# Order of the three partial products in a block product, of low parts and joins on VectorE, and the place of the sinks' load in a hybrid attention and recurrence block

## The chip, the cores and the metric

The kernel runs on one core of one Trainium2 chip. The metric is the device time of one execution in microseconds (us); a lower time is better. Five engines work side by side and meet through semaphores: TensorE (PE, its weight loads PEld), VectorE (DVE), ScalarE (ACT), GpSimd (POOL) and SyncE (SP), which issues most DMAs. Each works through its own queue in order.

## The reference

One residual block of a decoder, 1024 tokens by 1024 channels, in float32. The part that takes most of the time is one input projection onto 6656 columns; its output is cut into attention (q, k, v), a recurrence (xr), two SiLU gates and two merge gates.

```python
h = rmsnorm(x, norm_g[l]) * (1.0 + scale[:, None, :]) + shift[:, None, :]
proj = h @ w_in[l]
q, k, v, g_attn, xr, g_rnn, m_attn, m_rnn = jnp.split(proj, SPLIT_POINTS, axis=-1)
...
y_attn = sliding_window_attention_with_sinks(q, k, v, attn_sinks[l]) * jax.nn.silu(g_attn)
xr = causal_depthwise_conv(xr, conv_w[l], conv_b[l])
y_rnn = rg_lru(xr, positions, rg_wa[l], rg_ba[l], rg_wx[l], rg_bx[l], rg_lambda[l]) * jax.nn.silu(g_rnn)
merged = (jax.nn.sigmoid(m_attn) * (y_attn @ w_attn_proj[l])
          + jax.nn.sigmoid(m_rnn) * (y_rnn @ w_rnn_proj[l]))
x = x + gate[:, None, :] * (merged @ w_out[l])
return rmsnorm(x, final_g)
```

The attention is over blocks of 128 tokens with 16 heads, a window of 128, and one learned sink for each head: the sink is one more logit in the maximum and in the denominator of the softmax, without a value.

```python
m = jnp.maximum(jnp.max(s, axis=-1, keepdims=True), sink)
p = jnp.exp(s - m)
denom = jnp.sum(p, axis=-1, keepdims=True) + jnp.exp(sink - m)
```

## The kernel before

**Arithmetic.** Every large matrix is split into a high part, a float32 rounded to TensorE's fp32r form, and a low part, the rest. A product is then three matmuls: high by high, low weight by high, high weight by low. For a tile of weights the high part `wh` is a cast on ScalarE (`cast`, L105, L107), the low part `wl` a subtraction on VectorE (`rest`, L111, L113) that reads `wh`. Both come from a ring of five buffers (`slot`).

**Input projection by block products.** Most of the projection is done in 23 pairs of 128-column chunks. A `Pair` is a 2 by 2 block product in seven multiplications instead of eight (Strassen's scheme in Winograd's form): sums S1 to S4 of the four weight blocks A11, A12, A21, A22 (`tsum`, L732, VectorE), and prepared sums of the activations. Each of the seven is one call of `product` (L703 to L712): four slices of 128 along the contraction, three matmuls each, twelve matmuls of 128x512 into one PSUM bank, all with their own weight load. The loop is over slices on the outside, and inside it takes high weights by high activations, low weights by high activations, high weights by low activations. The first matmul of a product needs `wh`, the second `wl`.

**Slots.** `run` (L843) walks a table of slots; a slot is one product on TensorE. After the product of slot t has been issued, the steps that were put down for t are issued in the order in which they were put there: weight loads, casts, sums, low parts, copies out of the banks, joins, sinks. A step is a tuple of its engine, its times for ScalarE and VectorE, and a function; the letter is not used for anything else. Behind them `background` issues steps of the recurrence, the rope tables and w_out as far as its estimate of each engine's load allows. The order in each engine's queue is the order of these calls (`manual_schedule`); only the output stage at the end is ordered by the scheduler, after its own model of the time.

**Joins.** The seven products of a pair accumulate in four banks bk0 to bk3. C11 is read as it stands (`b1`), with a bank copy on ScalarE (L762); C12 and C22 are differences of a bank and a block kept in SBUF (`join`, L770, VectorE). A join waits for TensorE's product, and what stands behind it in VectorE's queue waits with it. The join of C12 reads the bank of product S4 (sixth of a pair), which the next pair's S1 (its second) overwrites; the join of C22 reads the bank of S3 (seventh), into which A22 adds in the next pair's third slot. What a pair's output is for decides the steps after a join ("sinks" of a pair, not to be confused with attention's): rope for q, tanh and a product (L830) for gates, convolution for xr.

**Attention.** After the last pair but one, `open_attn` opens new pools in memory that the recurrence has left, loads keys, queries, the sinks (16 numbers to all partitions, issued by GpSimd) and values, and 32 units follow, one for each key-value group and block of 128 tokens, interleaved with the last pair's seven products and then with the recurrence's projection. For a unit u: GpSimd copies four sinks into the last column of the tile `p` (`sink`, L1315); TensorE makes the scores (L1327); ScalarE copies them beside the sinks (L1336); VectorE merges the window (L1342), or for the first block of a group GpSimd masks it (L1345, select); VectorE takes the negative maximum (L1347); ScalarE the exponentials (L1352); then the division, transposes, splits and values.

**Constants.** `pk_t` (128 x 96) holds small columns for every channel, loaded at the start. Its columns 8 to 15 (`PK_BSH`) and 16 to 23 (`PK_BSC`) are the biases of shift and scale; they are read in the start stage alone, by `scales_of` and by one sum into `bng`.

The tile names of the profile: `bk` a bank, `wh`, `wl` the parts of weights, `r` a raw weight tile, `ws` a sum of blocks, `hh`, `hl`, `nh`, `nl` the parts of activations, `c` an output block, `u`, `p` kept blocks (`p` is attention's tile too), `s_ps` scores.

Of the kernel before, what the change touches and what calls it, by code (L numbers as in the profile page):

```python
# [12 lines left out]
F32 = mybir.dt.float32  # L13
# [9 lines left out]
P = 128  # L23
S = 1024
D = 1024
KC = 8
HALF = 512
NH = 16
# [26 lines left out]
def tile_hybrid_block(ctx, tc, x, pk, rows, posr, posi, c_row, w_ss, w_gate, w_main, w_v,  # L55
# [53 lines left out]
    def rest(dst, src, scale=1.0):  # L109
        if scale == 1.0:  # L110
            V.tensor_tensor(out=dst[1][:], in0=src, in1=f32(dst[0][:]), op=ALU.subtract)  # L111
        else:
            V.scalar_tensor_tensor(out=dst[1][:], in0=src, scalar=scale, in1=f32(dst[0][:]),  # L113
                                   op0=ALU.mult, op1=ALU.subtract)
# [463 lines left out]
    W = {}  # L578
# [78 lines left out]
    fixed = {}  # L657
# [46 lines left out]

    def product(ps, w, b, first=True):
        h, l = w
        for kc in range(4):
            c = slice(kc * P, (kc + 1) * P)
            for i, (ww, xx_) in enumerate(((h, 0), (l, 0), (h, 1))):
                W["pe"] = T.matmul(ps, ww[:, c], b[kc][xx_],  # L710
                                   start=(first and kc == 0 and i == 0),
                                   stop=(kc == 3 and i == 2), skip_group_check=not first)  # L712

    class Pair:
        def __init__(self, c, sinks, scale=1.0):
# [2 lines left out]
        def place(self, s, par, last):  # L718

            b1, b2, b3 = bk[0], bk[1 + par], bk[3]  # L720
            R, O, sc = {}, {}, self.scale
            self.ops, self.banks = O, (b1, b2, b3, bk[2 - par])

            def load(n):
                i, j = int(n[1]) - 1, int(n[2]) - 1
                return "S", 0, 0, lambda: R.__setitem__(
                    n, load_half(w_main[self.c + i][:, SL[j]]))

            def tsum(dst, a, b, op):
                def f():  # L730
                    R[dst] = wp.tile([P, HALF], F32, tag="ws", name="ws", bufs=3)[:]
                    V.tensor_tensor(out=R[dst], in0=R[a], in1=R[b], op=op)  # L732
                return "D", 0, 0.69, f

            def hi(n):
                def f1():
                    O[n] = slot()
                    cast(O[n], R[n], sc)
                return "A", 0.62, 0, f1

            def lo(n):
                return "D", 0, 0.69, lambda: rest(O[n], R[n], sc)

            SUB, ADD = ALU.subtract, ALU.add
            at_slot(s - 6, [load("A11"), load("A21")], load("A22"), load("A12"))
            at_slot(s - 2, [hi("A11"), tsum("S1", "A21", "A22", ADD)],
                    [hi("S1"), lo("A11"), tsum("S2", "S1", "A11", SUB)],
                    [lo("S1"), tsum("S3", "A21", "A11", SUB)],
                    hi("S2"),
                    [hi("A12"), lo("S2"), tsum("S4", "S2", "A12", SUB)],  # L750
                    [hi("S4"), lo("A12")], [hi("S3"), lo("S4")], lo("S3"))
            at_slot(s + (5 if last else 7), hi("A22"), lo("A22"))

            T_ = {}

            def keep(n, src):
                def f():
                    T_[n] = stp.tile([P, HALF], F32, tag=n, name=n)
                    A.copy(T_[n][:], src)
                return "A", 0.58, 0, f  # L760

            at_slot(s + 1, ("A", 0.58, 0, lambda: A.copy(b1, b2)))  # L762
            at_slot(s + 2, keep("p5", b3))
            at_slot(s + 4, keep("u2", b2))
            at_slot(s + 5, *self.sinks["C11"](lambda: b1))

            def join(out_, n, a, b):
                def f():
                    T_[n] = out_()
                    V.tensor_tensor(out=T_[n], in0=a(), in1=b(), op=SUB)  # L770
                return "D", 0, 0.69, f

            d12, k12 = self.sinks["C12"]
            d22, k22 = self.sinks["C22"]
            at_slot(s + 6, join(d12, "C12", lambda: T_["u2"][:], lambda: b3),
                    *k12(lambda: T_["C12"]))
            at_slot(s + 7, join(d22, "C22", lambda: b2, lambda: T_["p5"][:]),
                    *k22(lambda: T_["C22"]))
            if last:
                def add():  # L780
                    V.tensor_tensor(out=T_["u2"][:], in0=T_["u2"][:], in1=self.banks[3], op=ADD)
                at_slot(s + 7, keep("u2", b2), ("D", 0, 0.69, add),
                        *self.sinks["C21"](lambda: T_["u2"][:]))
            else:
                at_slot(s + self.sinks.get("late", 10), *self.sinks["C21"](lambda: b2))
# [61 lines left out]
    def run(pairs, extra):  # L847

        n = len(pairs)
        for t in range(-6, 7 * n + 14):  # L850
            i, k = divmod(t, 7)
            q = {0: (0, "A11", B11, 1, True), 1: (0, "S1", NT1, 2, True),
                 2: (-1, "A22", NT4, 1, False), 3: (0, "S2", T2, 1, False),
                 4: (0, "A12", B21, 0, False), 5: (0, "S4", B22, 2, False),
                 6: (0, "S3", NT3, 1, False)}[k]
            if t == 7 * n:
                q = -1, "A22", NT4, 3, True
            d = 0.0
            if 0 <= i + q[0] < n and t <= 7 * n:
                d = extra()  # L860
                p = pairs[i + q[0]]
                product(p.banks[q[3]], p.ops[q[1]], q[2], q[4])
                d += SLOT
            W["slot"] = t
            for st_ in fixed.pop(t, ()):
                put(st_)
            if d:
                background(d)
                Load.pe += d
            if d or t > 7 * n:  # L870
                yield
# [404 lines left out]
    def open_attn():  # L1276
        nonlocal at, psx
        psm_ctx.close()
        psx = pool(psx_ctx, "psx", space=PSUM)
        W["kq"] = pool(at_ctx, "kq", bufs=2, side="right")  # L1280
        W["yo"] = pool(at_ctx, "yo", side="right")
        W["pp"] = pool(at_ctx, "pp", bufs=3, side="right")
        W["pp"].tile([P, 56], F32, name="pad", bufs=1)
        at = pool(at_ctx, "at", side="right")
        load_kq(0)
        W["sink"] = W["pp"].tile([P, NH], F32, name="sink", bufs=1)
        dma(W["sink"][:], rows[0:1, 2048:2048 + NH].to_broadcast([P, NH]), G)
        load_v(0)
        load_kq(1)

# [21 lines left out]
    def sink(u):  # L1312
        px = U["p", u] = W["pp"].tile([P, 4, P + 1], F32, tag="p", name="p")
        gs = slice(u // 8 * 4, u // 8 * 4 + 4)
        G.tensor_copy(px[:, :, P:P + 1], W["sink"][:, gs].unsqueeze(2))  # L1315

    def scores(u):
        g, n = u // 8, u % 8
# [320 lines left out]
    b12_ctx.close()  # L1639
    Load.act = Load.dve = 0.0  # L1640

    W["vpp"] = pool(rope_ctx, "vp", side="right")
    for g in range(NG):
        v_prep(g)
# [397 lines left out]
```

## Time and profile before

| | |
|---|---|
| three timed runs | 914.56, 915.07, 917.21 us, median 915.07 |
| the profiled execution | 917.52 us, its span 915.8 us |
| granted TensorE clock, mean | 0.997 |
| matmuls, of them in block products | 4259, 1932 |
| TensorE's matmuls busy | 899.3 us, 98% |
| VectorE busy | 717.0 us, 78% |
| ScalarE busy | 566.0 us, 62% |
| GpSimd busy | 130.5 us, 14% |
| DMA, mean over the span | 197 GB/s |

The span goes from the first to the last instruction; the execution's own time has 1.7 us more around it. The stages follow one another: start and norm up to about 60 us, the first projections and v up to 92, the block products of 23 pairs up to about 592 with the recurrence between them, attention from 564 to 740 with the recurrence's projection between its units, the attention projection and the merge up to 832, then the output projection and the last norm. In a row of a timeline the columns are start, duration, engine, line, operation, output and inputs, shapes and count; the bracket at the end is the idle time of that engine ahead of the row and who ended it. In a row of waits they are who waited, for whom, and then the total, the count and the longest.

### The profile page before, as it was taken

What the parts mean: (1) busy time and instruction counts of PE and PEld (TensorE: products, weight loads), DVE (VectorE), ACT (ScalarE), POOL (GpSimd) and SP (SyncE); (2) the same over time, 40 slices, a digit from 0 to 9 for tenths busy, and PEclk for the clock granted to TensorE, in tenths of its full rate; (3) what the DMA queues carried; (4) which work ended last, traced back from release to release, by engine and by line L of the source; (5) the groups of instructions that cost most, each with busy time, mean ns of one, the idle gap of its engine ahead of it and who ended that gap; (6) DMA issues with size and microseconds to landing.
All of it is one profiled execution on the core that took longest, in us unless ns stands there. A gap on an engine that the chain in (4) does not pass through costs nothing.

```text
span 915.8 us, 12572 instructions
## 1 busy us (share of the span) xinstructions
PE 899.3 (98%) x4259; PEld 745.9 (81%) x4259; DVE 717.0 (78%) x1071; ACT 566.0 (62%) x1102; POOL 130.5 (14%) x216
## 2 busy tenths in 40 slices
PE   8999999999999999999999999999999999999996
PEld 6789888788888788878888887888888888888885
DVE  6997687888669865987788596899999946678855
ACT  7965554645566755776495884788888733115435
POOL 6520241200000000000000001253444400000000
PEclk9999999999999999999999999999999999999999
DMA  9828489772435353353546257996665279416504
GB/s 356 330 77 274 171 266 302 242 237 94 149 127 190 129 199 120 127 185 123 173 154 211 104 177 264 309 384 240 196 216 204 93 284 378 142 46 230 207 1 184
DMA packets 87204, 180.72 MB, mean 197 GB/s; under 512 B 8626, under 2 KB 29122, under 8 KB 87140
## 3 DMA queue, kind: packets, MB, share of 16 engines
q1 hardware_dynamic: 83056, 167.07, 51.9%
q0 software_dynamic: 3936, 12.59, 4.4%
q8 instruction: 33, 0.54, 0.2%
q14 instruction: 31, 0.25, 0.1%
q10 hardware_dynamic: 148, 0.27, 0.1%
HBM read 121.34 MB, written 58.95 MB: 197 GB/s over the span
## 4 chain that ended last, share of the span: by engine, by line
issue 44%; PE 41%; DVE 9%; ACT 3%; DMA 2%; POOL 1%; SPq 0%; DVEq 0%; POOLq 0%; ACTq 0%
PE rp L173 13%; PE out L1855 6%; PE pmain L173 5%; PE bk L710 4%; PE s_ps L1327 3%; PE pv L1400 2%; PE pmain L485 2%; PE bk L485 2%; PE pt L1366 1%; DMA wr<-w_gate 1%; PE pmain L1577 1%; PE pmain L1576 1%; PE pmain L1575 1%; DVE wl L113 1%; DVE wl L111 1%
## 5 line engine op out<-in xcount | busy, mean ns | idle before, releaser
L710 PE MATMUL bk<-nh,wl 128*128 128x512 f32 x368 | 144.4, 392 | 2.8 <-DVE wl L111 2.8
L710 PE MATMUL bk<-nh,wh 128*128 128x512 f32 x368 | 144.1, 392 | 0.0
L710 PE MATMUL bk<-nl,wh 128*128 128x512 f32 x368 | 143.9, 391 | 0.0
L111 DVE TENSOR_TENSOR wl<-r,wh 128x512 fp32r<-128x512 f32 x109 | 78.9, 731 | 8.7 <-ACT wh L105 8.7
L710 PEld LDWEIGHTS bk<-nh,wl 128*128 128x128 f32 x368 | 69.5, 189 | 19.0 <-DVE wl L111 4.4
L105 ACT CAST wh<-r 128x512 fp32r<-128x512 f32 x107 | 65.6, 618 | 30.6 <-PE rp L173 10.0
L710 PEld LDWEIGHTS bk<-nh,wh 128*128 128x128 f32 x368 | 69.5, 189 | 14.5 <-ACT bk L762 0.2
L710 PEld LDWEIGHTS bk<-nl,wh 128*128 128x128 f32 x368 | 69.4, 189 | 14.3
L710 PE MATMUL bk<-hh,wl 128*128 128x512 f32 x184 | 72.1, 392 | 0.4 <-DVE wl L111 0.4
L710 PE MATMUL bk<-hl,wh 128*128 128x512 f32 x184 | 71.6, 389 | 0.0
L710 PE MATMUL bk<-hh,wh 128*128 128x512 f32 x184 | 71.6, 389 | 0.0
L111 DVE TENSOR_TENSOR wl<-ws,wh 128x512 fp32r<-128x512 f32 x76 | 51.9, 684 | 4.0 <-ACT wh L105 4.0
L62 POOL DMA_DIRECT2D yh_d<-av x1 | 0.6, 567 | 373.9 <-ACT av L1086 373.9
L1352 ACT ACTIVATE p<-p,small 128x129 f32<-128x129 f32 x128 | 50.1, 401 | 0.3 <-DVE small L1347 0.3
L105 ACT CAST wh<-ws 128x512 fp32r<-128x512 f32 x76 | 46.0, 614 | 3.3 <-PE bk L710 2.1
L710 PEld LDWEIGHTS bk<-hh,wl 128*128 128x128 f32 x184 | 34.5, 188 | 9.0 <-DVE wl L111 1.5
L710 PEld LDWEIGHTS bk<-hh,wh 128*128 128x128 f32 x184 | 34.5, 188 | 7.1
L710 PEld LDWEIGHTS bk<-hl,wh 128*128 128x128 f32 x184 | 34.5, 188 | 7.0
L1327 PE MATMUL s_ps<-ks,qs 128*128 128x256 f32 (+1 forms) x256 | 37.6, 289 | 0.4 <-DMA qs<-q_d 0.2
L710 PE MATMUL bk<-hha,wl 128*128 128x512 f32 x92 | 36.2, 393 | 1.7 <-DVE wl L111 1.0
L823 ACT ACTIVATE c<-bk 128x512 f32<-128x512 f32 x29 | 17.3, 596 | 31.2 <-PE bk L710 31.2
L710 PE MATMUL bk<-hha,wh 128*128 128x512 f32 x92 | 35.9, 390 | 0.0
(375 smaller groups left out, 2321.3 us busy)
## 6 DMA issues: line engine op xcount, KB each, us to landing
r<-w_main SPq DMA_DIRECT2D x100, 256.0 KB, 4.4
wada<-w_ss SPq DMA_DIRECT2D x16, 512.0 KB, 9.0
qs<-q_d SPq DMA_DIRECT2D x16, 512.0 KB, 5.5
wo_d<-wr SPq DMA_DIRECT2D x28, 256.0 KB, 2.8
wo<-wo_d SPq DMA_DIRECT2D x14, 512.0 KB, 5.5
ks<-k_d SPq DMA_DIRECT2D x12, 384.0 KB, 4.3
xt<-x SPq DMA_DIRECT2D x8, 512.0 KB, 7.2
sma_d<-c SPq DMA_DIRECT2D x16, 256.0 KB, 4.7
```

Of the source, the lines that this page charges most:

```text
L105: A.copy(dst[0][:], src)
L111: V.tensor_tensor(out=dst[1][:], in0=src, in1=f32(dst[0][:]), op=ALU.subtract)
L113: V.scalar_tensor_tensor(out=dst[1][:], in0=src, scalar=scale, in1=f32(dst[0][:]), op0=ALU.mult, op1=ALU.subtract)
L173: mm = T.matmul(ps[hf], ww, xx[kc][hf], start=(kc == 0 and ww is w_h and xx is xh), stop=(kc == KC - 1 and xx is xl))
L485: T.matmul(starts[c][hf], ww[:, c0:c0 + P], xh[kc][hf], start=(kc == 0 and t_ == "h"), stop=(kc == KC - 1 and t_ == "l"))
L710: W["pe"] = T.matmul(ps, ww[:, c], b[kc][xx_], start=(first and kc == 0 and i == 0), stop=(kc == 3 and i == 2), skip_group_check=not first)
L823: A.activation(t["t"], s(), AF.Tanh, scale=0.5)
L1327: W["pe"] = T.matmul(o, qs[:, j, qc], ks[:, kb:n % 2 + 2, b, :], start=(b == 0), stop=(b == 1))
L1352: A.activation(px[:, j, :], px[:, j, :], AF.Exp, bias=sm[:, 0, j:j + 1], accum_out=sm[:, 1, j:j + 1])
L1366: W["pe"] = T.transpose(pt[:, j, :], px[:, j, 0:P], ident[:])
L1400: W["pe"] = T.matmul(pv[:], b, m[:].rearrange("p j q -> p (j q)"), start=(i == 0), stop=(i == len(prods) - 1))
L1855: T.matmul(o, a[k][x_][:, p * P:(p + 1) * P], b[k][y_][:, cols], start=(first and k == 0 and i == 0), stop=(k == 3 and i == 2), skip_group ...
```

## The change

Three edits. `product` runs the high weights over all four slices first, each slice with the high and then the low part of the activations, and then the low weights over the four slices: the first eight matmuls need `wh` only, the last four `wl`. `lo`, the step that makes a low part, gets the letter "L" for "D", and `run` sorts the steps of a slot so that those with "L" come first, all others in their old order. The sinks are loaded right after the start stage into columns 8 to 23 of `pk_t`, and attention copies them from there; the tile `sink` is gone, and a pad of 56 columns ahead of attention's tiles grows by its 16 columns to 72, so that the other tiles stay where they were.

```diff
     def product(ps, w, b, first=True):
         h, l = w
-        for kc in range(4):
-            c = slice(kc * P, (kc + 1) * P)
-            for i, (ww, xx_) in enumerate(((h, 0), (l, 0), (h, 1))):
-                W["pe"] = T.matmul(ps, ww[:, c], b[kc][xx_],
-                                   start=(first and kc == 0 and i == 0),
-                                   stop=(kc == 3 and i == 2), skip_group_check=not first)
+        terms = [(h, kc, i) for kc in range(4) for i in range(2)] + [(l, kc, 0) for kc in range(4)]
+        for n, (ww, kc, i) in enumerate(terms):
+            W["pe"] = T.matmul(ps, ww[:, kc * P:(kc + 1) * P], b[kc][i],
+                               start=(first and n == 0), stop=(n == 11),
+                               skip_group_check=not first)
...
             def lo(n):
-                return "D", 0, 0.69, lambda: rest(O[n], R[n], sc)
+                return "L", 0, 0.69, lambda: rest(O[n], R[n], sc)
...
             W["slot"] = t
-            for st_ in fixed.pop(t, ()):
+            for st_ in sorted(fixed.pop(t, ()), key=lambda s_: s_[0] != "L"):
                 put(st_)
...
-        W["pp"].tile([P, 56], F32, name="pad", bufs=1)
+        W["pp"].tile([P, 72], F32, name="pad", bufs=1)
         at = pool(at_ctx, "at", side="right")
         load_kq(0)
-        W["sink"] = W["pp"].tile([P, NH], F32, name="sink", bufs=1)
-        dma(W["sink"][:], rows[0:1, 2048:2048 + NH].to_broadcast([P, NH]), G)
         load_v(0)
...
-        G.tensor_copy(px[:, :, P:P + 1], W["sink"][:, gs].unsqueeze(2))
+        G.tensor_copy(px[:, :, P:P + 1], pk_t[:, PK_BSH:PK_BSH + NH][:, gs].unsqueeze(2))
...
     b12_ctx.close()
     Load.act = Load.dve = 0.0
 
+    dma(pk_t[:, PK_BSH:PK_BSH + NH], rows[0:1, 2048:2048 + NH].to_broadcast([P, NH]), G)
     W["vpp"] = pool(rope_ctx, "vp", side="right")
```

On TensorE, a product of the last pair, between the scores (`s_ps`) of attention's second and third unit; before:

```order
L710 MATMUL bk_69<-nh_751,wh 128x512
L710 MATMUL bk_69<-nh_751,wl 128x512
L710 MATMUL bk_69<-nl,wh 128x512
L710 MATMUL bk_69<-nh_752,wh 128x512
L710 MATMUL bk_69<-nh_752,wl 128x512
L710 MATMUL bk_69<-nl,wh 128x512
L710 MATMUL bk_69<-nh_753,wh 128x512
L710 MATMUL bk_69<-nh_753,wl 128x512
L710 MATMUL bk_69<-nl,wh 128x512
L710 MATMUL bk_69<-nh_754,wh 128x512
L710 MATMUL bk_69<-nh_754,wl 128x512
L710 MATMUL bk_69<-nl,wh 128x512
```

The same twelve after the change:

```order
L709 MATMUL bk_69<-nh_751,wh 128x512
L709 MATMUL bk_69<-nl,wh 128x512
L709 MATMUL bk_69<-nh_752,wh 128x512
L709 MATMUL bk_69<-nl,wh 128x512
L709 MATMUL bk_69<-nh_753,wh 128x512
L709 MATMUL bk_69<-nl,wh 128x512
L709 MATMUL bk_69<-nh_754,wh 128x512
L709 MATMUL bk_69<-nl,wh 128x512
L709 MATMUL bk_69<-nh_751,wl 128x512
L709 MATMUL bk_69<-nh_752,wl 128x512
L709 MATMUL bk_69<-nh_753,wl 128x512
L709 MATMUL bk_69<-nh_754,wl 128x512
```

The first use of `wl` has moved from second to ninth place; the four of `wl` now run one behind the other.

On VectorE, where attention begins: `small` is the negative maximum of the first unit, `c<-c` a gate's product (L830, after the change L829), and the `wl` behind it the low part of the product above; before:

```order
L770 TENSOR_TENSOR c<-bk_70,p_5164 128x512
L111 TENSOR_TENSOR wl<-ws,wh 128x512
L732 TENSOR_TENSOR ws<-r 128x512
L111 TENSOR_TENSOR wl<-r,wh 128x512
L830 SCALAR_TENSOR_TENSOR c<-c 128x512
L1258 TENSOR_TENSOR wr<-wr 128x512
L1347 TENSOR_REDUCE small<-p 128x4
L830 SCALAR_TENSOR_TENSOR c<-c 128x512
L111 TENSOR_TENSOR wl<-ws,wh 128x512
L732 TENSOR_TENSOR ws<-ws,r 128x512
```

After the change:

```order
L111 TENSOR_TENSOR wl<-ws,wh 128x512
L769 TENSOR_TENSOR c<-bk_70,p_5165 128x512
L731 TENSOR_TENSOR ws<-r 128x512
L111 TENSOR_TENSOR wl<-r,wh 128x512
L829 SCALAR_TENSOR_TENSOR c<-c 128x512
L1257 TENSOR_TENSOR wr<-wr 128x512
L1344 TENSOR_REDUCE small<-p 128x4
L111 TENSOR_TENSOR wl<-ws,wh 128x512
L829 SCALAR_TENSOR_TENSOR c<-c 128x512
L731 TENSOR_TENSOR ws<-ws,r 128x512
```

Two low parts have passed what stood ahead of them in their slot, a join and a gate's product; the maximum, which belongs to attention and to no slot, still stands ahead of the second.

On GpSimd, at the same place, before:

```order
L62 DMA yl_d_128<-it 128x1024
L62 DMA sink<-rows 128x16
L62 DMA vd<-vd_d_85 128x128
L62 DMA vd<-vd_d_85 128x256
L1315 COPY p<-sink 128x4
L1345 AFFINE_SELECT p<-p 128x4x128
```

After the change:

```order
L62 DMA yl_d_128<-it 128x1024
L62 DMA vd<-vd_d_85 128x128
L62 DMA vd<-vd_d_85 128x256
L1312 COPY p<-pk_t 128x4
L1342 AFFINE_SELECT p<-p 128x4x128
```

The load of the sinks is gone here; it now stands behind the loads of the rope tables (`ctab`, `stab`) and ahead of that of the positions (`pos`). In the output stage, which the scheduler orders, a few bank copies and weight casts of ScalarE and their partners on VectorE have changed places; TensorE's order there is the same.

## The prediction

> **What bounds the kernel now.** I read the page first: its head and the engines' busy time.
>
> ```profile
> span 915.8 us, 12572 instructions
> ...
> PE 899.3 (98%) x4259; PEld 745.9 (81%) x4259; DVE 717.0 (78%) x1071; ACT 566.0 (62%) x1102; POOL 130.5 (14%) x216
> ```
>
> TensorE is busy for 98% of the span, but that figure hides stalls: a matmul's record lasts 0.39 us while the next starts 0.23 us later, so the tail of one record covers a short hole. The spacing of starts counts. The waits of the weight loads (PEld) show the holes, since every matmul here has a load of its own.
>
> ```profile
> engine line waited for: us in total, times, longest us
> PEld bk L710 <- DVE wl L111: 7.8, 10, 2.2
> ...
> PEld bk L710 <- DVE wl L113: 1.8, 3, 1.1
> ```
>
> So 13 loads in the block products (L710) waited 9.6 us for VectorE's low part `wl`. What such a wait costs is read from one of them, the longest but one, in the timeline:
>
> ```profile
> 401.63 0.39 PE L710 MATMUL bk<-hha,wh 128*128 128x512 f32 x1
> 401.69 0.67 DVE L770 TENSOR_TENSOR c<-u,bk 128x512 f32<-128x512 f32 x1
> 402.27 0.69 DVE L111 TENSOR_TENSOR wl<-r,wh 128x512 fp32r<-128x512 f32 x1
> ...
> 403.01 0.19 PEld L710 LDWEIGHTS bk<-hha,wl 128*128 128x128 f32 x1 [1.41 <-DVE wl L111]
> 403.01 0.50 PE L710 MATMUL bk<-hha,wl 128*128 128x512 f32 x1 [0.99 <-DVE wl L111]
> ...
> 403.36 0.40 PE L710 MATMUL bk<-hla,wh 128*128 128x512 f32 x1
> ```
>
> The first matmul of a product starts at 401.63, the third at 403.36: 1.73 us for two steps of 0.227 us. The loss is 1.28 us, 0.13 to 0.14 less than the load's wait of 1.41. VectorE stood in a join (L770) and only then made the low part that TensorE wanted as its second matmul. The last view is the timeline where attention begins, with the longest wait.
>
> ```profile
> 559.75 0.55 POOL L62 DMA_DIRECT2D sink<-rows  x1
> 560.28 1.07 POOL L62 DMA_DIRECT2D vd<-vd_d  x2
> ...
> 565.24 0.59 ACT L1336 COPY p<-s_ps 128x512 f32<-128x512 f32 x1 [3.45 <-PE s_ps L1327]
> ...
> 568.37 0.19 POOL L1315 COPY p<-sink 128x4 f32<-128x4 f32 x1 [7.01 <-DMA sink<-rows]
> 568.51 0.64 POOL L1345 TENSOR_SCALAR_AFFINE_SELECT p<-p 128x512 f32<-128x512 f32 x1
> 568.81 0.39 PE L710 MATMUL bk<-nh,wh 128*128 128x512 f32 x1
> 569.01 0.59 ACT L1336 COPY p<-s_ps 128x512 f32<-128x512 f32 x1 [2.18 <-PE s_ps L1327]
> ...
> 569.18 0.69 DVE L1347 TENSOR_REDUCE small<-p 128x4 f32<-128x516 f32 x1 [6.77 <-POOL p L1345]
> 569.79 0.68 DVE L830 SCALAR_TENSOR_TENSOR c<-c 128x512 f32<-128x512 f32 x1
> 569.91 0.40 ACT L1352 ACTIVATE p<-p,small 128x129 f32<-128x129 f32 x1 [0.31 <-DVE small L1347]
> ...
> 570.39 0.69 DVE L111 TENSOR_TENSOR wl<-ws,wh 128x512 fp32r<-128x512 f32 x1
> ...
> 571.13 0.50 PE L710 MATMUL bk<-nh,wl 128*128 128x512 f32 x1 [1.93 <-DVE wl L111]
> ...
> 571.86 0.63 PE L710 MATMUL bk<-nh,wh 128*128 128x512 f32 x1
> 572.28 0.63 PE L710 MATMUL bk<-nh,wl 128*128 128x512 f32 x1
> ...
> 575.35 1.11 PE L1327 MATMUL s_ps<-ks,qs 128*128 128x256 f32 x8
> 576.50 0.59 ACT L1336 COPY p<-s_ps 128x512 f32<-128x512 f32 x1 [3.94 <-PE s_ps L1327]
> 577.11 0.74 DVE L1342 COPY_PREDICATED p<-mgt,s_ps 128x512 f32<-128x512 uint32 x1 [2.58 <-ACT p L1336]
> ```
>
> The sinks' load, issued at 559.75, lands as late as 568.3. GpSimd's copy waits for it, then its select, then VectorE's maximum, and behind that in VectorE's queue the low part of the product that began at 568.81. After the hole of 1.93 us the matmuls start 0.42 us apart instead of 0.23. That one product lasts from 568.81 to 575.35, 6.54 us where twelve steps take 2.72.
>
> **The product's order.** The same twelve matmuls run, so the first question is their spacing. High part first means that the same `wh` slice is loaded twice in a row. The projections of the late stages do that already (each slice for two halves), and stand in the chain beside block products of the old order:
>
> ```profile
> 576.46 2.75 PE bk L710 x12
> ...
> 788.62 10.88 PE rp L173 x48
> ```
>
> Twelve matmuls take 2.75 us in the one and 10.88 / 4 = 2.72 in the other. I cost the new spacing at nothing; the bounds are the difference of the two rows either way, 0.03 us on each of 161 products, 4.8 us up or down, and zero is taken because an undisturbed product of either order is nearest to its 2.72.
>
> What moves is the need for `wl`: from the second matmul to the ninth, 7 x 0.227 = 1.59 us later. Every wait but the longest lost less (1.28 at most), so each fits inside by itself. Where two follow closely they add up, as here, 10 us ahead of the row at 403:
>
> ```profile
> 393.47 0.19 PEld L710 LDWEIGHTS bk<-hh,wl 128*128 128x128 f32 x1 [0.83 <-DVE wl L111]
> ```
>
> Without this hole (0.83 - 0.14) TensorE would start the later product at 400.94 and its ninth matmul at 402.76, while `wl` is ready at 402.96 in the old order. The second edit decides this place: with the low part ahead of the join it runs from 401.7 to 402.4. The loss of the twelve shorter waits is 9.6 - 2.2 = 7.4 us of waiting less 12 x 0.14, so **5.7 us**, and all of it should go.
>
> **Low parts ahead of joins.** Work is only permuted within a slot, 0.69 us for each low part (row 402.27). The sums (L732) that feed the next high part keep the same work ahead of them, and ScalarE's order stays up to the output stage. What is queued behind a moved low part is a join or a rope step. A join frees a PSUM bank, which TensorE overwrites two products after the last matmul that the join reads, so it has about 5.4 us. From 100 to 575 us VectorE's waits are these:
>
> ```profile
> DVE c L770 <- PE bk L710: 26.2, 13, 6.3
> ...
> DVE wl L111 <- ACT wh L105: 4.5, 4, 1.7
> ```
>
> VectorE stood 26.2 us in joins that waited for TensorE, with low parts behind them; that standing is filled now. In the other direction, a low part waits for ScalarE's cast 1.7 us at the longest. A join then comes 1.7 + 0.69 us later and takes 0.69: 3.1 us of 5.4. Cost: nothing; what it costs if that cover is gone stands with the slower rival.
>
> In the output stage the scheduler moves a bank copy behind a weight cast. The copy with the least to spare is the fourth:
>
> ```profile
> 849.90 0.58 ACT L1900 COPY out<-out 128x512 f32<-128x512 f32 x1
> ...
> 851.02 0.62 PE L1855 MATMUL out<-wo,mh 128*128 128x512 f32 x2
> ```
>
> It ends 0.54 us ahead of the matmul. The same work still lies ahead of it, so I count nothing, with up to 0.5 us of loss for the range.
>
> **Sinks early.** The load moves to GpSimd's queue behind the rope tables:
>
> ```profile
> 55.26 0.97 POOL L62 DMA_DIRECT2D stab<-cs_d  x2
> 90.58 0.57 POOL L62 DMA_DIRECT2D pos<-posi  x1 [34.35 <-DMA v_d<-vv]
> ```
>
> Its issue of 0.55 us falls into 34 us in which GpSimd waits anyway, and its first reader comes at 561, so even a landing after 8.6 us is hidden: zero. At the attention start the copy can run once the two `vd` loads are issued, at 561.35. The select waits for ScalarE's copy (565.24 + 0.59) and runs 565.9 to 566.5; the maximum follows to 567.2, and the low part, now ahead of L830, ends at 567.9. TensorE wants it at 568.81 + 1.82 = 570.6: 2.7 us to spare, no hole, no slow pace. So 6.54 - 2.72 = **3.8 us** go. Late next would be ScalarE: its copy at 569.01 waits for scores that do not move, so its exponentials (569.91) gain the 0.31 us before them, while TensorE gains 3.8. The idle 3.94 us at 576.50 and VectorE's 2.58 at 577.11 take that up, and both come out just in step.
>
> [...] The row: 1.93 us of idleness, and half the pace follows at once. [...]
>
> **The sum.** 5.7 + 3.8 = 9.5 us. The profiled execution took 917.5 us (its span 915.8 and 1.7 around it), so 908.0 in its terms. The three timed runs read 914.56, 915.07 and 917.21: two lie 2.5 us below it, one beside it. Either profiling adds that, and 915.1 - 9.5 = 905.6 follows; or some runs have a shorter hole at 571 and no slow pace, which cannot be removed twice, and 908.0 stands. I take the middle, **906.8 us**.
>
> **The rivals.**
>
> *The attention start is mostly absent from timed runs, or its slow pace has another cause.* For it: the spread of the three runs is about the slow pace and a part of the hole. [...] Against it: one run of three lies at 917.21. Then only the 5.7 come off the median: 909.4.
>
> *VectorE becomes the bound.* The holes may only have shown that it was late.
>
> ```profile
> 580.00:730.00 150.00, 149.68 (x826) 127.92 (x826) 138.75 (x254) 124.98 (x402) 64.58 (x105) 1.00 0.67 234
> ```
>
> In attention it is busy for 138.75 of 150 us. Against it: TensorE loses only 0.3 us in that stretch, and elsewhere VectorE has the 26 us of joins to give. If all the holes of the products come back and only the attention start is won: 915.1 - 3.8 = 911.3.
>
> *The new order is spaced wider*, by the 0.03 us of its bound. For it: the row of 2.75; against it: 2.72 with doubled loads. That returns 4.8 us: 910.4, or 914.2 if the attention start is absent too.
>
> *Joins come too late, and the kernel is slower.* A low part now holds the queue while it waits for its cast, and the join behind it frees the bank. It decides once that wait exceeds 5.4 - 0.69 - 0.69 = 4.0 us, and 1.7 was the longest. If one join in each of 22 pairs held TensorE by one operation of 0.69 us, 15.2 us would stand against the 9.5 won: 915.1 + 5.7 = 920.8.
>
> **How the numbers follow.** Forecast 0.55, attention start absent 0.18, VectorE bound 0.10, wider spacing 0.11, joins 0.04, a gain larger than the sum 0.02. What a measurement of this kernel can tell from no change is 0.3%, 2.7 us: faster is below 912.3, slower above 917.8. All but the joins and 0.06 of the spacing (with the attention start absent) are faster: 0.90; the same 0.06; slower 0.04. The range begins at 904.6, the sum against the median less 1 us for small waits in attention that I left in, and ends at 911.5, behind VectorE's case.
>
> **What would show it.** Right: no load of a block product waits for `wl`; the product at the attention start takes 2.72 us up to the next scores; the copy of the sinks follows the `vd` issues by less than 1 us; no spacing of 0.42 us after the first 5 us; twelve matmuls still take 2.72 to 2.75. Wrong: weight loads that now wait for ScalarE's cast, products that wait for a join (L769) or a bank copy (L761), or a twelve of 2.8 us or more. A total above 912.3 with the holes gone would mean that time is lost in attention or the output stage.

## The result and the profile after

| | median, us | runs | before beside it | ratio, 95% interval |
|---|---|---|---|---|
| the change | 911.17 | 6 (910.13 to 912.80) | 916.22, 6 runs | 0.9950 (0.9936 to 0.9963) |

The kernel became faster, by 5.05 us in the medians. The forecast was 906.8 us, from gains that add up to 9.5 us; about half of that sum came. The profiled execution took 911.87 us; its span fell from 915.8 to 910.2.

The page's head and the engines' busy time:

```profile
span 910.2 us, 12600 instructions
...
PE 896.9 (99%) x4258; PEld 746.8 (82%) x4259; DVE 718.4 (79%) x1071; ACT 566.6 (62%) x1102; POOL 128.7 (14%) x216
```

The waits of the weight loads and of the matmuls, where the 13 waits for `wl` stood before:

```profile
PEld pv L1397 <- POOL plm L1383: 1.6, 4, 0.5
...
PE s_ps L1324 <- DMA qs<-q_d: 2.5, 1, 2.5
```

No block product (now L709) waits for `wl` any more. In their place stands one wait, of the first scores (L1324) for the queries' load, 2.5 us. The chain of waits shows where that load hangs; its columns are start, duration and what ran:

```profile
353.59 51.45 PE bk L709 x227
...
550.08 0.61 DVE c L829
...
550.71 0.38 SPq L62
...
551.14 0.46 SPq L62
...
551.65 0.44 SPq L62
...
552.26 0.32 SPq L62
...
552.63 7.28 DMA qs<-q_d
...
560.04 1.08 PE s_ps L1324 x8
561.12 4.40 PE bk L709 x12
565.52 0.95 PE s_ps L1324 x8
566.47 2.75 PE bk L709 x12
```

Three things are to be read here. The first row: 227 matmuls in 51.45 us, 0.227 us each, so high part first costs nothing in spacing. Then the chain leaves TensorE: a gate's product on VectorE (L829) releases its store to `ga_d` on SyncE's queue; behind that store stand two stores to `wo_d`, the keys, and the queries, whose load takes 7.28 us from issue to landing. Last, the product behind the first scores takes 4.40 us, where the one behind it takes 2.75. The granted clock says why (PEclk is the column behind the busy times):

```profile
561.70:565.10 3.40, 3.40 (x9) 2.61 (x8) 2.49 (x4) 1.05 (x3) 0.92 (x3) 0.50 1.03 395
```

For 3.4 us TensorE had half its clock, 0.50, much as in the trace of before behind its hole, 0.54:

```profile
571.80:575.20 3.40, 3.40 (x10) 2.61 (x9) 2.59 (x5) 0.75 (x2) 0.00 (x0) 0.54 0.99 288
```

The sinks are out of the way, as forecast:

```profile
554.95 1.73 POOL L1312 COPY p<-pk_t 128x4 f32<-128x4 f32 x1
...
561.82 0.64 POOL L1342 TENSOR_SCALAR_AFFINE_SELECT p<-p 128x512 f32<-128x512 f32 x1 [5.14 <-ACT p L1333]
...
563.10 0.68 DVE L111 TENSOR_TENSOR wl<-ws,wh 128x512 fp32r<-128x512 f32 x1
```

GpSimd's copy waits for no DMA, the select waits for ScalarE, and the low part is ready at 563.78.

Five stages account for the difference. "Ready" is the start of the last matmul ahead of the first scores plus 0.227; all other marks are starts of matmuls in the timelines.

| profiled execution | first block product | to ready | wait for the first scores | first to third scores | third to last scores |
|---|---|---|---|---|---|
| before | 91.75 | 471.99 | 0.38 | 11.23 | 144.02 |
| the change | 91.36 | 466.07 | 2.61 | 9.01 | 144.63 |

The block products gave 5.9 us. At the attention start 2.2 us were won behind the first scores and 2.2 lost ahead of them. Attention lost 0.6; the start gained 0.4; the rest is 0.1. Together 5.9 + 0.4 + 2.2 - 2.2 - 0.6 - 0.1 = 5.6, the difference of the spans.

### The profile page after: what moved, and what is told of

Its sections match the earlier page's. It is cut to its first block, busy times and chain, and to the rows that moved or that the text cites. A ratio compares the mean times of both kernels' runs of the same rounds, so it can differ in the third digit from the quotient of the medians.

```text
span 910.2 us, 12600 instructions
## 1 busy us (share of the span) xinstructions
PE 896.9 (99%) x4258; PEld 746.8 (82%) x4259; DVE 718.4 (79%) x1071; ACT 566.6 (62%) x1102; POOL 128.7 (14%) x216
## 4 chain that ended last, share of the span: by engine, by line
PE 91%; DVE 5%; ACT 2%; issue 1%; DMA 1%; POOL 0%; SPq 0%; DVEq 0%; ACTq 0%
PE bk L709 47%; PE rp L173 13%; PE out L1853 6%; PE pmain L173 5%; PE pgate L1022 5%; PE s_ps L1324 3%; PE pv L1397 2%; PE pmain L485 2%; PE bk L485 2%; PE pt L1363 1%; PE pmain L1574 1%; PE pmain L1573 1%; PE pmain L1572 1%; DMA qs<-q_d 1%; ACT jk L1871 1%
## 5 line engine op out<-in xcount | busy, mean ns | idle before, releaser
L709 PE MATMUL bk<-nl,wh 128*128 128x512 f32 x368 | 143.9, 391 | 0.0
L709 PE MATMUL bk<-nh,wh 128*128 128x512 f32 x368 | 143.8, 391 | 0.0
L709 PE MATMUL bk<-nh,wl 128*128 128x512 f32 x368 | 99.0, 391 | 0.0
L709 PEld LDWEIGHTS bk<-nh,wl 128*128 128x128 f32 x368 | 69.6, 189 | 14.6
L709 PEld LDWEIGHTS bk<-nh,wh 128*128 128x128 f32 x368 | 69.4, 189 | 14.5
L709 PEld LDWEIGHTS bk<-nl,wh 128*128 128x128 f32 x368 | 69.3, 188 | 14.3
L709 PE MATMUL bk<-hl,wh 128*128 128x512 f32 x184 | 71.6, 389 | 0.0
L709 PE MATMUL bk<-hh,wh 128*128 128x512 f32 x184 | 71.6, 389 | 0.0
L709 PE MATMUL bk<-hh,wl 128*128 128x512 f32 x184 | 49.2, 389 | 0.0
L709 PEld LDWEIGHTS bk<-hh,wl 128*128 128x128 f32 x184 | 34.5, 188 | 7.2
L709 PEld LDWEIGHTS bk<-hh,wh 128*128 128x128 f32 x184 | 34.6, 188 | 7.1
L709 PEld LDWEIGHTS bk<-hl,wh 128*128 128x128 f32 x184 | 34.5, 188 | 7.1
L1324 PE MATMUL s_ps<-ks,qs 128*128 128x256 f32 (+1 forms) x256 | 37.6, 289 | 2.7 <-DMA qs<-q_d 2.5
L709 PE MATMUL bk<-hha,wh 128*128 128x512 f32 x92 | 35.8, 389 | 0.0
L709 PE MATMUL bk<-hla,wh 128*128 128x512 f32 x92 | 35.8, 389 | 0.0
L1324 PEld LDWEIGHTS s_ps<-ks,qs 128*128 128x128 f32 x256 | 32.4, 189 | 3.7 <-issue 2.8
```

What stands on the lines that cost most here:

```text
L709: W["pe"] = T.matmul(ps, ww[:, kc * P:(kc + 1) * P], b[kc][i], start=(first and n == 0), stop=(n == 11), skip_group_check=not first)
L1324: W["pe"] = T.matmul(o, qs[:, j, qc], ks[:, kb:n % 2 + 2, b, :], start=(b == 0), stop=(b == 1))
```

## The experiments

The theory was formed from this trace: the queries' load is the next lock at the attention start, that is, what TensorE waits for there once the hole is gone; it hangs on SyncE's queue and on its own time in flight, 6.6 us from issue to landing before and 7.3 with the change. So what TensorE gains ahead of it is waited away, and the third edit removes a wait that the queries now cover. The rivals were that the half pace belongs to the place and not to a wait, that VectorE's order decides, or that something else is as late there.

Every experiment was timed beside the kernel before (medians 915.87, 916.05 and 915.89 in the three groups e1 to e4, e5 to e8, e9 and e10). The stages of their profiled executions, as above:

| | first block product | to ready | wait for the first scores | first to third scores | third to last scores |
|---|---|---|---|---|---|
| e1 order only | 91.98 | 466.86 | 1.88 | 9.00 | 144.04 |
| e2 order, low parts | 91.71 | 466.04 | 2.05 | 7.46 | 144.84 |
| e3 sinks only | 91.30 | 471.80 | 1.12 | 7.41 | 144.05 |
| e4 change, queries early | 91.41 | 466.11 | 0 | 7.37 | 144.02 |
| e5 as e4, sinks late | 91.22 | 466.41 | 0 | 7.37 | 144.03 |
| e6 change, wait filled | 92.94 | 466.04 | 2.27 of filling | 7.35 | 144.03 |
| e7 before, queries early | 91.76 | 472.19 | 0 | 7.37 | 144.04 |
| e8 change, stores behind | 91.30 | 466.08 | 0 | 7.37 | 144.73 |
| e9 as e5, low parts behind joins | 91.52 | 466.79 | 0 | 7.37 | 144.03 |
| e10 as e4, with a wait | 92.94 | 466.04 | 2.10 | 7.41 | 144.68 |

### e1: the product's order alone

```diff
-        for kc in range(4):
...
+        terms = [(h, kc, i) for kc in range(4) for i in range(2)] + [(l, kc, 0) for kc in range(4)]
```

> Only the product's order is changed; low parts stay behind joins, the sinks are loaded where they were. Theory Q (keys and queries are the next lock): the waits for wl of the block products up to 550 us go, about 6 us, but TensorE then reaches the first scores ahead of the queries and waits for qs about 2 us, and the product behind still waits for wl, because the sinks' load still lands about 8 us after its issue; so about 3 us faster than before, between 911 and 914. Rival O (the order of products alone brings all of the change): as fast as the whole change, about 5 us faster. Rival V (VectorE's order is what counts): no gain without the low parts ahead.

Measured: 911.98 us, ratio 0.9959 (0.9947 to 0.9971), 3.9 us faster. The waits of the weight loads in its profile:

```profile
PEld s_ps L1326 <- issue: 2.1, 1, 2.1
...
PEld bk L709 <- DVE wl L111: 1.1, 3, 0.6
```

Three waits for `wl` are left, 1.1 us, two of them close to each other at 400 and 403 us (the first row is the wait for the queries, which the weight load of the scores shares). The block products took 5.1 us less than before. No wait for `wl` stood behind the first scores: the expectation was wrong there, since the product that reads this low part now wants it as its ninth matmul. Rival V is out. Rival O, that the order alone brings the whole change, is not parted from theory Q by the totals (the interval of the change is 0.9936 to 0.9963); the trace has the wait of 1.88 us for the queries that theory Q named.

### e2: low parts ahead as well

```diff
-                return "D", 0, 0.69, lambda: rest(O[n], R[n], sc)
+                return "L", 0, 0.69, lambda: rest(O[n], R[n], sc)
...
-            for st_ in fixed.pop(t, ()):
+            for st_ in sorted(fixed.pop(t, ()), key=lambda s_: s_[0] != "L"):
```

> Product order and low parts ahead of joins, the sinks loaded where they were. Theory Q: 0 to 1 us faster than the product order alone (the one or two places where a low part still came late, and 0.7 us at the attention start), and slower than the whole change by the hole behind the sinks, 1 to 3 us. Rival: no difference to the whole change, if the early sinks bring nothing.

Measured: 910.93 us, ratio 0.9948 (0.9931 to 0.9964): as fast as the whole change, although the sinks load late again. Its timeline at the attention start:

```profile
559.80 1.08 PE L1326 MATMUL s_ps<-ks,qs 128*128 128x128 f32 x8 [1.89 <-DMA qs<-q_d]
...
563.24 0.19 POOL L1314 COPY p<-sink 128x4 f32<-128x4 f32 x1 [8.02 <-DMA sink<-rows]
...
564.47 0.40 PE L709 MATMUL bk<-nh,wh 128*128 128x512 f32 x1
564.67 0.68 DVE L111 TENSOR_TENSOR wl<-ws,wh 128x512 fp32r<-128x512 f32 x1
...
566.31 1.07 PE L709 MATMUL bk<-nh,wl 128*128 128x512 f32 x4
```

GpSimd waited 8.02 us for the sinks, and the low part was made as late as 564.67 to 565.35. But the product that wants it began at 564.47, because TensorE had waited for the queries, and took the low part at 566.31, 1.0 us later than it was ready. On top of the other two edits, the third is worth nothing that these intervals show. Half the clock did not come here, behind 2.05 us of waiting: it was 1.00 from 560.7 to 564 us.

### e3: the sinks alone

```diff
-        W["sink"] = W["pp"].tile([P, NH], F32, name="sink", bufs=1)
-        dma(W["sink"][:], rows[0:1, 2048:2048 + NH].to_broadcast([P, NH]), G)
...
+    dma(pk_t[:, PK_BSH:PK_BSH + NH], rows[0:1, 2048:2048 + NH].to_broadcast([P, NH]), G)
```

> Only the sinks are loaded early; products and low parts as before. Theory Q: TensorE reaches the first scores no earlier than before, so its wait for qs stays at 0.4 us, and the hole of 2.1 us with the half pace behind it, 3.8 us together, goes: 3.5 to 4 us faster, about 912. Rival P (the half pace belongs to the attention start whatever precedes it): 2 us faster, and steps of 0.42 us are still there. Rival N (the hole was not in the timed runs): less than 1 us.

Measured: 913.87 us, ratio 0.9980 (0.9968 to 0.9991), 2.0 us faster and not 3.8. In its chain the first scores and the products behind them:

```profile
557.35 6.74 DMA qs<-q_d
...
564.22 1.08 PE s_ps L1325 x8
565.30 2.79 PE bk L710 x12
568.09 0.95 PE s_ps L1325 x8
569.04 2.75 PE bk L710 x12
```

The hole and the slow product are gone, as theory Q had it. But TensorE was ready at 563.10, 0.64 us earlier than in the trace of before, while the queries landed no sooner: the wait grew from 0.38 to 1.12. The queries were the next lock already in the kernel before. The median gains less than the 3.8 us that left the trace. A part, 0.7 us, goes into that wait. The rest is argued, not shown: the half pace (1.6 us of it) may not be in every execution, for the traced execution of before took 917.52 us, 1.65 more than the median of before beside e3.

### e4: keys and queries early

Keys and queries lie in memory that the seventh row of the recurrence gives up about 18 us before they are loaded. The tiles of that row got a pool of their own (`rr_ctx`), which closes two slots after the row's last store; the first four loads follow at once.

```diff
+        W["rr"] = pool(rr_ctx, "rnn2", side="right")
...
-        W["kq"] = pool(at_ctx, "kq", bufs=2, side="right")
...
-        load_kq(0)
         load_v(0)
-        load_kq(1)
...
+    def open_kq():
+        if "kq" not in W and W["slot"] >= W.get("free", 999) + 2:
+            rr_ctx.close()
+            W["kq"] = pool(at_ctx, "kq", bufs=2, side="right")
+            load_kq(0)
+            load_kq(1)
```

> The change, and the keys and queries of the first four units are loaded about 17 us earlier, as soon as the seventh row of the recurrence has given up its memory. Theory Q: the first scores wait for nothing, the half pace behind them goes with the wait, 2.6 + 1.6 = 4.2 us: about 907.0, 8 to 9 us faster than before. Rival P (half pace without a wait): 908.5. Rival D (something else is as late as the queries there, values, VectorE or the low part): less than 1 us faster than the change, with a new wait in the place of qs.

Measured: 907.61 us, ratio 0.9915 (0.9902 to 0.9928), 8.3 us faster than before; e5 and e9, which also have the queries early, are not parted from it, and no version has a lower median. Its chain:

```profile
557.68 0.84 PE s_ps L1331 x8
558.52 2.83 PE bk L709 x12
561.35 0.95 PE s_ps L1331 x8
562.30 2.75 PE bk L709 x12
```

Nothing waits at the attention start, and no product there is slow: the clock was 1.00 from 557 to 570 us. Theory Q holds, rival D falls, and so does rival P: in this trace the place alone brought no half pace. Against the trace of the change the span is 4.7 us shorter, against its median the time 3.6.

### e5: the same with the sinks late

The same edit, with the sinks loaded by GpSimd just ahead of the values, as in the kernel before.

```diff
-        G.tensor_copy(px[:, :, P:P + 1], pk_t[:, PK_BSH:PK_BSH + NH][:, gs].unsqueeze(2))
+        G.tensor_copy(px[:, :, P:P + 1], W["sink"][:, gs].unsqueeze(2))
```

> Product order, low parts ahead and keys and queries early, but the sinks loaded where they were before. Theory Q2 (the early sinks bring nothing once the products take the high part first, since the low part behind the maximum is wanted only 1.6 us later, and the sinks land sooner when no queries are in flight): as fast as with the early sinks, 907 to 908.5, and no wait for wl behind the first scores. Rival S (the sinks were hidden by the wait for the queries alone): the hole comes back, 1 to 3 us slower, 909 to 911.

Measured: 907.71 us, ratio 0.9906 (0.9893 to 0.9920); no difference to e4. On GpSimd:

```profile
555.78 0.55 POOL L62 DMA_DIRECT2D sink<-rows  x1
...
559.57 0.19 POOL L1321 COPY p<-sink 128x4 f32<-128x4 f32 x1 [2.17 <-DMA sink<-rows]
```

Without the queries in flight the sinks landed 3.7 us after their issue and not 8.6. Rival S falls: once the product takes the high part first, no gain of the early sinks is seen, with a wait for the queries (e2) or without.

### e6: the wait filled with work

```diff
         s_ps = s_full[:].rearrange("p (j k) -> p j k", j=4)
+        for _ in range(10 if u == 0 else 0):
+            T.matmul(s_full[:, 0:HALF], hh[0][0][:, 0:P], hh[0][0], start=True, stop=True)
```

> The change, with ten matmuls of 128x512 on old operands (their result is overwritten) ahead of the first scores, 2.3 us of work in the 2.6 us of waiting for the queries. Theory W (the half pace comes from the idle time just before it): no steps of 0.42 us behind the first scores, the mean granted clock 0.997 or more as with the early queries, and 1 to 1.6 us faster than the change, 909.5 to 910. Rival X (the half pace belongs to the place, or to chance): the clock stays at 0.994 to 0.997, and the time at 911 or, where the queries land early, above it.

Measured: 910.69 us, ratio 0.9937 (0.9924 to 0.9951), mean clocks 0.996 to 0.998 where the change had 0.994 to 0.997. The clock of the start stage and of the attention start (PEclk is the third entry behind the stretch):

```profile
24.00:28.00 4.00, 3.73 (x9) 0.57 1.04 407
558.00:570.00 12.00, 12.00 (x66) 1.00 1.00 354
```

At the attention start the clock stayed full. In this execution it was halved in the start stage instead, where the trace of the change shows 1.00. The intervals of e6 and the change overlap: inconclusive as a gain.

### e7: queries early in the kernel before

The edit of e4 in the kernel before, with nothing else.

```diff
+        if "kq" not in W and W["slot"] >= W.get("free", 999) + 2:
+            rr_ctx.close()
```

> The kernel before, with nothing of the change, but keys and queries of the first four units loaded about 17 us earlier. Theory C (the sinks landed 8.6 us late because the queries' megabytes were in flight): the sinks land about 4 us after their issue, the hole of 2.1 us and the half pace go, and the 0.4 us of waiting for the queries: 3.5 to 4.2 us faster than before, about 912. Rival L (the sinks are late by the load's own duration): the hole stays, at most 0.4 us faster.

Measured: 913.79 us, ratio 0.9974 (0.9964 to 0.9984), 2.3 us faster. On GpSimd, and the sinks' load in the list of issues (8 KB, 3.5 us to landing):

```profile
sink<-rows POOLq DMA_DIRECT2D x1, 8.0 KB, 3.5
```

```profile
563.88 0.19 POOL L1322 COPY p<-sink 128x4 f32<-128x4 f32 x1 [1.99 <-DMA sink<-rows]
565.65 0.64 POOL L1352 TENSOR_SCALAR_AFFINE_SELECT p<-p 128x512 f32<-128x512 f32 x1 [1.58 <-ACT p L1343]
```

The sinks landed in 3.5 us, the select waited for ScalarE and no longer for them, and the hole went although the sinks were loaded as late as ever. Theory C holds: the sinks were late, 8.6 us to landing in the kernel before, because of the bytes around them. Again it is 2.3 us by the median, where the trace of before has 4.2 us of losses at the attention start.

### e8: two stores behind the queries

```diff
-                    dma(wo_d[j][k], at(n))
+                    if W["slot"] < 150 or "kq" in W:
+                        dma(wo_d[j][k], at(n))
+                    else:
+                        held.append((wo_d[j][k], at(n)))
...
         load_v(0)
+        while held:
+            dma(*held.pop(0))
         load_kq(1)
```

> The change, with two stores of 256 KB to wo_d put behind the first keys and queries in SyncE's queue instead of ahead of them. Theory B (the queries wait for the bytes ahead of them: 0.95 us of issue and 0.5 MB at about 0.38 MB per us, 1.3 us): the queries land 2.3 us earlier, the first scores wait 0.3 us instead of 2.6, and the time falls by 2.3 us and by the half pace where it was, to 908 to 909. Rival I (only the issue counts): 1 us of the wait goes, about 910. Rival F (the load takes 7 us from wherever it is issued, and something else holds the issue): no gain.

Measured: 909.57 us, ratio 0.9922 (0.9909 to 0.9934). SyncE's queue and the queries' load in the list of issues:

```profile
549.91 0.38 SPq L62 DMA_DIRECT2D ga_d<-c  x1
550.46 0.33 SPq L62 DMA_DIRECT2D ks<-k_d  x1
550.85 0.44 SPq L62 DMA_DIRECT2D qs<-q_d  x1
551.34 1.29 SPq L62 DMA_DIRECT2D wo_d<-wr  x2
```

```profile
qs<-q_d SPq DMA_DIRECT2D x1, 512.0 KB, 6.2
```

The queries were issued 1.8 us earlier than with the change (550.85 against 552.63; 0.8 of it because the store to `ga_d` itself came earlier) and needed 6.2 us instead of 7.3. They landed at 557.0 and TensorE was ready at 557.38: no wait. In the trace issue and bytes ahead both count, as theory B had it. The total does not settle it: 909.57 lies between the 908 to 909 of theory B and the 910 of rival I, and the traced execution is the fastest of the five.

### e9: low parts behind joins, queries early

e5 without the letter "L" and the sort.

```diff
-            for st_ in sorted(fixed.pop(t, ()), key=lambda s_: s_[0] != "L"):
+            for st_ in fixed.pop(t, ()):
```

> Product order and early keys and queries; low parts behind joins and the sinks' load as before. Theory L (low parts ahead are worth only the place at 400 us, where the run of the product order alone still lost 0.6 us in two products): 0.5 to 1 us slower than with the low parts ahead (907.7), 908.2 to 908.7. Rival L0 (the new order alone covers all): 907.7. Rival L2 (VectorE's order also decides at the attention start): 2 us slower or more, with a wait for wl behind the first scores.

Measured: 908.00 us, ratio 0.9910 (0.9892 to 0.9929). The waits in its profile:

```profile
PEld bk L709 <- DVE wl L111: 1.1, 3, 0.6
```

The block products take 0.4 us longer than in e5 and 0.7 longer than in e4. The medians agree with that size (0.3 and 0.4 us); the intervals don't part them, and only the three waits in the trace speak against rival L0. Rival L2 is out: at the attention start VectorE's order decides nothing.

### e10: a wait on purpose

```diff
+        for _ in range(6 if u == 0 else 0):
+            G.memset(px[:, :, 0:P], 0.0)
         G.tensor_copy(px[:, :, P:P + 1], pk_t[:, PK_BSH:PK_BSH + NH][:, gs].unsqueeze(2))
...
+        if u == 0:
+            T.transpose(s_full[:, 0:P], U["p", 0][:, 0, 0:P], ident[:])
```

> The change with early keys and queries (907.6), and on purpose a wait of about 2.2 us ahead of the first scores: TensorE first transposes a tile that GpSimd fills six times over (the result is overwritten). No DMA is waited for. Theory W (idle time of 2 us brings half the pace behind it in most executions): 2.2 us and on average 1 us or more behind them, 910.8 to 911.4, clock 0.994 to 0.997, steps of 0.42 us behind the wait. Rival X (the half pace belonged to the crowded DMA or to the place): only the wait, 909.8, clock 0.997 to 0.999, all steps 0.23.

Measured: 911.44 us, ratio 0.9942 (0.9924 to 0.9959), 3.8 us more than e4 by the medians and 2.5 by the ratios, for a wait of 2.1. The wait, and then the clock of the start stage and behind the wait:

```profile
560.98 0.33 PE L1331 MATMUL s_ps<-ident,p 128*128 128x128 f32 x1 [1.84 <-POOL p L1320]
```

```profile
24.00:28.00 4.00, 3.74 (x9) 0.57 1.04 409
561.00:565.00 4.00, 4.00 (x23) 1.00 0.69 184
```

In the profiled execution the clock stayed full behind the wait and was halved in the start stage. Of the six runs two took 910.09 and 910.26 us at a mean clock of 0.997 and 0.998, four 911.3 to 912.1 at 0.996. So the total that theory W named came, but not by its way in the traced execution: its span is 4.1 us longer than e4's, of which 2.1 is the wait, 1.5 the start stage with its halved clock and 0.7 a loss later in attention, less 0.2 elsewhere. That idle time just before brings the half pace is not shown here.

## Why the prediction was half right

**The block products' 5.7 us: right.** 5.9 by the trace. The order alone brings 5.1 of it. Low parts ahead bring 0.4 to 0.8 (e1 against e2, e9 against e4 and e5), mostly around 400 us, where the prediction saw two waits add up; there e1 has waits of 0.6 and 0.4 us, where the prediction's times leave 0.2 (402.96 against 402.76).

**Zero for the spacing, the joins and the output stage: right.** Starts are 0.227 us apart before and after, no product waits for a join, and from the last scores to the end of the span 196.4 us became 196.5. The rivals of wider spacing and late joins did not happen.

**The attention start's 3.8 us: the step that failed.** The hole behind the sinks went, but the sentence "Late next would be ScalarE" was wrong. Late next were the queries, and the trace of before has them; these are its issue of that load, the load in the list of issues (its last column is from issue to landing), and the first scores:

```profile
557.41 0.59 SPq L62 DMA_DIRECT2D qs<-q_d  x1
```

```profile
qs<-q_d SPq DMA_DIRECT2D x1, 512.0 KB, 6.6
```

```profile
564.12 0.64 PE L1327 MATMUL s_ps<-ks,qs 128*128 128x128 f32 x4 [0.22 <-DMA qs<-q_d]
```

A wait of 0.2 us looked like nothing. It meant that this load had no slack at all, and TensorE was about to be ready 6.3 us earlier (5.9 by the products and 0.4 by the start). The issue moved by 4.8 us only (557.41 to 552.63), because the store ahead of it waits for VectorE (L829, 0.61 us from 550.08), and the load took 7.3 us instead of 6.6. So the landing moved by 4.1, and 2.2 of the 6.3 us were waited away. That wait took the place of the hole in full: it delayed the product long enough for even the late sinks (e2), and the half pace came behind it. Where 7.37 us from first to third scores are undisturbed (e4), the losses at the attention start were 0.38 + 3.86 = 4.2 us before and 2.61 + 1.64 = 4.2 after.

**The half pace as a sure part of the stall: wrong in size.** About 1.6 of the 3.8 us (eight steps of 0.42 us instead of 0.227) were counted as if each execution had them. e3 and e7, which remove the hole without hurrying TensorE, gain 2.0 and 2.3 us by their medians. And the clock does differ between executions of one kernel: of the eleven runs of before beside e9 and e10, five had a mean clock of 0.996 and took 917.3 us on average, four had 0.998 and took 915.3; in the other two groups the runs at 0.998 are shorter than those at 0.996 as well, by 1.8 us (against a single run) and 0.8. Which stage was halved in them is not on record. The rival that part of the attention start is absent from timed runs was probably right in this, though not in what came of it.

**VectorE as the bound: a small part.** The total, 911.17, is close to the 911.3 of this rival, but by luck: the holes of the products did not come back. Attention lost 0.6 us more than before. VectorE is nearly full there, in the change (29.01 us of the 30 from 595 to 625) as in before (28.98 of the same stretch, 601 to 631). The loss appears in four of the eleven changed kernels (the change, e2, e8, e10: 144.63 to 144.84 us from third to last scores, where the others and before have 144.02 to 144.05). Where 0.46 us of it arise in the change, 40 us behind the third scores, two instructions meet, a select on GpSimd and attention's division on VectorE. In the change, and then in e4, which has no such loss:

```profile
609.55 0.63 POOL L1383 TENSOR_SCALAR_AFFINE_SELECT phm<-phc 128x512 fp32r<-128x512 f32 x1 [0.82 <-ACT phc L1368]
609.57 1.15 DVE L1356 TENSOR_TENSOR p<-p,small 128x512 f32<-128x512 f32 x1
```

```profile
605.29 0.69 DVE L1363 TENSOR_TENSOR p<-p,small 128x512 f32<-128x512 f32 x1
605.39 1.09 POOL L1390 TENSOR_SCALAR_AFFINE_SELECT phm<-phc 128x512 fp32r<-128x512 f32 x1 [0.82 <-ACT phc L1375]
```

In the change VectorE comes to its division 40.5 us behind the third scores; the select starts first, by 0.02 us, and the division takes 1.15 us. In e4 and in before (division at 615.76, select at 615.81) it comes there at 40.4, starts first by 0.10 and 0.05 and takes 0.69, and the select takes 1.09 and 1.14 instead of 0.63. So in these traces a delay of 0.1 us goes with 0.46 us more on an engine that is busy for 29 of 30 us. What delays VectorE in the change stays open, and that the meeting makes the loss was not tested by a run.

With the right next lock the sum would have been 5.9 for the products and nothing at the attention start: 911.6 in the profiled execution's terms, 911.87 measured. That it comes out so closely is partly luck: the 0.4 us gained at the start and the 0.6 lost in attention nearly cancel, and the losses at the attention start are equal before and after only in these two traces (3.5 us in e1, 2.1 in e2).

## What to carry to other kernels

The load whose wait was 0.2 us was the next lock here: before a stall's price is added to a gain made ahead of it, move TensorE forward by that gain and look at every landing on its way, however short its wait is now. The two waits at the attention start did not add up, with losses of 4.2 us there before and 4.2 after; removing one was worth what the other left. And the place of the queries' load was set by its memory and its queue, not by its reader: the buffers were free about 18 us earlier, and issuing the load then (534.5 us in e4, 552.63 in the change) brought 3.6 us more than the change did.

## What the runs showed of the hardware that was not expected

Half the granted clock for 3.4 us, at 0.43 us for 512 columns, came behind waits of 1.9 to 2.6 us at the attention start in three profiled executions (before, the change, e1: mean clocks of 0.54 from 571.8 to 575.2 us, 0.50 from 561.7 to 565.1, 0.66 from 561 to 566), and not behind 2.05 and 2.0 in two others (e2, e10: 1.00 from 560.7 to 564 and from 561 to 565). The start stage has holes of 0.8 and 0.4 us (beyond the spacing of 0.227) one behind the other at 22 to 24 us in before and in the change. There the clock from 24 to 28 us was 0.66, 0.71, 0.57 and 0.57 in e1, e2, e6 and e10, and 1.00 in before, the change and e4. So the length of the wait does not decide alone.

The clock records of before and of the change say more. The half clock at the attention start lasted 3.413 us in both, and each stretch at full clock that ends in a lower one a whole multiple of that: 566.61 and 337.92 us in before (166 and 99 times), 556.37 and 341.33 us in the change (163 and 100 times). In the 3.41 us ahead of the half clock TensorE was busy for 1.48 us in before (568.08 to 571.49) and for 1.67 in the change (558.30 to 561.71). These are two executions, and the clock fell in both; what decides whether it falls behind a wait is not shown by these runs.

A load of 8 KB from GpSimd, the sinks, landed 8.6 us after its issue with the queries' loads in flight (before), and 3.5 and 3.7 us after it without them (e7, e5).
